# Weight sums of a block-matrix scheme: made on VectorE in SBUF, or by adding transfers in DRAM

## The chip, the cores and the metric

The kernel runs on one core of one Trainium2 chip. Five engines run side by side, each through its own list of instructions in order: TensorE (PE: matmul; PEld: its weight loads), VectorE (DVE), ScalarE (ACT), GpSimd (POOL) and SyncE (SP), which here issues transfers only. Transfers (DMA) are carried out by 16 DMA engines, which all issuing engines share. The metric is the device time of one execution in microseconds (us), lower is better.

## The reference

One layer of an encoder over 2048 tokens of width 1024, all float32: chunked softmax attention with 16 heads of 64, then a SwiGLU feed-forward of width 2816, each between two RMS norms.

```python
def reference(x, g_pre_mix, g_post_mix, w_qkv, w_o, rel_bias, g_pre_ffn, g_post_ffn, w_gate, w_up, w_down):
    for i in range(DEPTH):                      # DEPTH = 1
        h = rms_norm(x, g_pre_mix[i])
        m = chunk_relpos_attention(h, w_qkv[i], w_o[i], rel_bias[i // N_MIXERS])
        x = x + rms_norm(m, g_post_mix[i])
        h = rms_norm(x, g_pre_ffn[i])
        x = x + rms_norm(swiglu(h, w_gate[i], w_up[i], w_down[i]), g_post_ffn[i])
    return x

def swiglu(h, w_gate, w_up, w_down):
    return (jax.nn.silu(h @ w_gate) * (h @ w_up)) @ w_down
```

In the attention, a chunk of 64 tokens reads its own and the eight chunks before it, with a learned bias by head and clipped distance added to the scores.

## The kernel before

Tokens are worked in two groups of 1024 (`g`), each of two halves of 512 (`s`). Every dense product is made of three matmuls (`products`, L188 to L190): each operand is split into a rounded part `hi` and a remainder `lo`, and hi·hi + hi·lo + lo·hi are added up in PSUM.

The feed-forward multiplies by a seven-product scheme for 2×2 block matrices: seven block products in place of eight. It needs four sums of the weights' blocks A11, A21, A22, A12, called S1 to S4, once per unit of weights. There are 17 units: eleven of the gate and up matrices, six of the down matrix, one of these of half width. Activations get sums of the same kind (T1 to T4), and the products are put together by further adds (`gate_up`, `down`).

The weight sums don't depend on the tokens, so they are made early, while the attention runs (first 1100 us), and are stored in DRAM (`sum_gu`, `sum_d`), from which the feed-forward loads them (L862, L880). One unit before the change: SyncE loads the four blocks into SBUF (`ws_A...`, L817), VectorE makes four sums in place (L820), SyncE stores the four results (L829).

What sets the order: TensorE's list is written out by hand. For each pair of heads `p` and each half `s` there is an `Attend` job of four slots (128 queries each). In a slot TensorE makes the scores of both heads into one PSUM bank `st` (L521, L522), VectorE adds the bias and finds the extreme (L530, out of the bank, which is then free for the next slot), ScalarE takes the exponential (L534), VectorE the reciprocal (L537), GpSimd normalises (L538), and TensorE transposes the result a slot later (L554, L565). Between these pieces dense matmuls (the q, k, v and output projections) are put in by a planner (`fill`). The other engines' lists are set by the framework's scheduler, from the order in which the program is written and its own estimate of when each instruction is ready.

The bias of a head is a tile of 128×640 that SyncE loads (L420) and in which GpSimd overwrites two corners (L421, L422). There are three such buffers and a pair of heads needs two, so the second tile of each pair can be loaded only when the pair before has made its last scores. Attention outputs are copied to one of three `io` tiles and stored by SyncE (L590).

The dense weights of the attention come in slabs: `fetch` (L119 on) loads slab `n` in two halves (`raw`, L139, one buffer) and splits it on ScalarE and VectorE. `take` hands out a slab and fetches the next. Behind the loads of certain slabs (`UNIT_AT`: 3 to 11 and 22 to 31) one unit of weight sums is written into the program.

Of the kernel before, what the change touches and what calls it, by code (L numbers as in the profile page):

```python
# [47 lines left out]
def trunk(  # L48
# [71 lines left out]
    def fetch():  # L120
        n = len(ready)
        if n == len(plan):
            return
        tiles = [w_tile(f"{n}_{c}") for c in range(2)]
        raw = None
        if n in roomy:

            raw = phase["ap"].tile([P, 4 * HALF], F32, tag="q", name=f"raw_{n}", bufs=2)
            sp.dma_start(raw, plan[n])
        for c in range(2):  # L130
            here = slice(c * 1024, c * 1024 + 1024)
            if n in roomy:
                part, ins = raw[:, here], None
            else:
                if "fp" in phase:
                    part = phase["fp"].tile([P, 1024], F32, tag="w4", name=f"raw_{n}_{c}", bufs=4)
                else:
                    part = wp.tile([P, 1024], F32, tag="raw", name=f"raw_{n}_{c}", bufs=1)
                ins = sp.dma_start(part, plan[n][:, here])  # L139
# [348 lines left out]
    class Attend:  # L488
# [14 lines left out]
        def scores(self, ib):  # L503
# [19 lines left out]
            for h in range(2):  # L523
# [14 lines left out]
                pool.tensor_scalar(  # L538
# [146 lines left out]
    class Blocks:  # L685
# [45 lines left out]
        def first(self, w):  # L731
# [28 lines left out]
        def all(self, w):  # L760
# [13 lines left out]
            def two(k):  # L774
                b11, b12, b22, b21 = c[k]
                t3 = narrow("t3")
                dve.tensor_tensor(t3, b22, b12, op=ALU.subtract)
                dve.tensor_tensor(b12, b12, b11, op=ALU.subtract)
# [3 lines left out]
            def three(k):  # L782
                b11, b12, b22, b21 = c.pop(k)
                dve.tensor_tensor(b22, b22, b12, op=ALU.subtract)
# [26 lines left out]
    def weight_sums(src, dst):  # L811

        t = {}

        def load(n):
            t[n] = phase["ap"].tile(list(src[n].shape), F32, tag="ws", name=f"ws_{n}", bufs=4)
            sp.dma_start(t[n], src[n])  # L817

        def add(out_, a, b, op):
            dve.tensor_tensor(t[out_], t[a], t[b], op=op)  # L820
# [5 lines left out]
        steps = [(0.5, lambda n=n: load(n)) for n in ("A11", "A21", "A22", "A12")]  # L826
        steps += [(2.0, lambda a=a: add(*a)) for a in sums]
        for n, at in (("S1", "A22"), ("S3", "A21"), ("S2", "A11"), ("S4", "A12")):
            steps.append((0.5, lambda n=n, at=at: sp.dma_start(dst[n], t[at])))  # L829
        return steps  # L830

    def gate_up_sums(c):
        return weight_sums({n: w_gu[c, BLOCK_AT[n]] for n in BLOCK_AT}, {n: sum_gu[n][:, c, :] for n in sum_gu})

    def down_sums(c):
        def at(t):
            return t[:, c, :] if c == 0 else t[:, c : c + 2, :].rearrange("p a b -> p (a b)")

        return weight_sums({n: at(w_d[BLOCK_AT[n]]) for n in BLOCK_AT}, {n: at(sum_d[n]) for n in sum_d})
# [57 lines left out]
    def gate_up(g, b):  # L897
# [20 lines left out]
        for c in range(NC):  # L918
# [21 lines left out]
            def closing(pts, terms, then):  # L940
                def go(i):
                    dve.tensor_tensor(terms[i], pts[i], terms[i], op=ALU.add)  # L942
# [8 lines left out]
            def sub(n, a, b_, to=None):  # L951
                t[n] = narrow(n) if to is None else to
                dve.tensor_tensor(t[n], a, b_, op=ALU.subtract)

            def c12(x_):
                t["B12"] = x_
                sub("T1", x_, t["B11"])
                put("T1")

            def c22(x_):  # L960
                t["B22"] = x_
                put("B22")
                sub("T3", x_, t["B12"], t["B12"])
                put("T3")
                sub("T2", x_, t["T1"])
                put("T2")

            def c21(x_):
                t["B21"] = x_
                put("B21")  # L970
                sub("T4", x_, t["T2"])
# [9 lines left out]
            yield from product(pc, "B22", False, closing(pc, u2, c12))  # L981
# [8 lines left out]
    def down(g, store, between=lambda n: None):  # L990
# [45 lines left out]
        def add(a, b_):  # L1036
            return lambda dst: dve.tensor_tensor(dst, a, b_, op=ALU.add)
# [17 lines left out]
        def u(d, _):  # L1055
            if not end:
                u2[d] = narrow("u2")
            dve.tensor_tensor(u2[d], pc[d], p1[d], op=ALU.add)
# [10 lines left out]
        def c22(d, _):  # L1069
            dve.tensor_tensor(u3[d], pc[d], p1[d], op=ALU.add)  # L1070
            store(1, 4 + d, whole, add(u3[d], p5[d]))
# [261 lines left out]
    units.extend(gate_up_sums(c) for c in range(NC))  # L1333
    units.extend(down_sums(c) for c in [0] + list(range(1, NC, 2)))
# [125 lines left out]
```

## Time and profile before

| what | value |
|---|---|
| time, median of 3 runs | 2495.56 us (2490.86 to 2497.91) |
| profiled execution: its time / its span | 2493.5 us / 2491.6 us |
| granted TensorE clock, mean | 0.990 |
| TensorE busy | 2418.1 us (97%) |
| VectorE busy | 1595.5 us (64%) |
| GpSimd busy | 328.7 us (13%) |
| weight sums on VectorE (L820) | 68 instructions, 85.5 us, from 90.4 to 927.4 us |
| their transfers (L817, L829) | 68 loads, 68 stores, all but 8 of 512 KB |
| DMA engines | 52.9% busy, 441.21 MB moved |

The profile is one execution, recorded by the hardware's profiler. Busy time of TensorE is partly modelled (matmuls are pipelined), so what counts is where it is idle and what it waited for. A row of a stretch gives for each engine the busy microseconds and the number of instructions, then the granted clock, the busy share of the DMA engines and GB/s. A row in order of time gives start, duration, engine, line, operation, out<-in, and in brackets the idle time just before it and who ended it.

### The profile page before, as it was taken

How to read it: one execution, taken by the hardware profiler on the slowest of the kernel's cores; microseconds unless marked ns; L12 is line 12 of the kernel's file. 1: busy time of each engine (PE TensorE's matmuls, PEld its weight loads, DVE VectorE, ACT ScalarE, POOL GpSimd, SP SyncE). 2: the span in 40 equal slices, each digit the busy share in tenths (PEclk: the TensorE clock that was granted, in tenths of full speed). 3: DMA queues.
4: the chain of work that ended last, by engine and by line, in shares of the span. 5: the costliest groups of instructions: out<-in, count | busy, mean ns of one | idle time of the engine just before them, and what ended most of it. 6: DMA issues, size and time to landing. Idle time of an engine off the chain costs nothing.

```text
span 2491.6 us, 34707 instructions
## 1 busy us (share of the span) xinstructions
PE 2418.1 (97%) x12536; PEld 1998.1 (80%) x12536; DVE 1595.5 (64%) x2698; ACT 1145.0 (46%) x1979; POOL 328.7 (13%) x428
## 2 busy tenths in 40 slices
PE   7999999999999999999999999999999999999997
PEld 5787877778878787877888788888888888888886
DVE  6766675658676755577666656577656655555576
ACT  5555554654565535464533243356443333334443
POOL 3232232211322222220000000000000000000002
PEclk9999999999999999999999999999999999999998
DMA  4545353445545441137666755377667664457653
GB/s 143 206 151 207 119 201 130 142 157 187 201 149 182 162 158 47 60 116 236 199 196 227 245 182 181 102 241 247 209 219 260 198 204 154 135 169 244 193 191 134
DMA packets 184316, 441.21 MB, mean 177 GB/s; under 512 B 20272, under 2 KB 22336, under 8 KB 182864
## 3 DMA queue, kind: packets, MB, share of 16 engines
q1 hardware_dynamic: 184144, 438.99, 52.9%
q8 instruction: 99, 1.62, 0.3%
q14 instruction: 73, 0.60, 0.1%
HBM read 325.09 MB, written 113.82 MB: 176 GB/s over the span
## 4 chain that ended last, share of the span: by engine, by line
PE 52%; DMA 1%; DVE 1%; issue 0%; ACT 0%; POOL 0%; SPq 0%; POOLq 0%; DVEq 0%; ACTq 0%
PE pd L189 5%; PE pd L188 5%; PE pd L190 5%; PE pb L188 5%; PE pb L189 5%; PE pb L190 5%; PE pa L188 3%; PE pa L189 3%; PE pa L190 3%; PE pc L188 3%; PE pc L189 3%; PE pc L190 3%; PE mm L188 1%; PE mm L190 1%; PE mm L189 1%; DMA res<-in_x 1%
## 5 line engine op out<-in xcount | busy, mean ns | idle before, releaser
L188 PE MATMUL mm<-hb,whi 128*128 128x512 f32 x720 | 299.2, 415 | 2.9 <-ACT hb L340 2.4
L534 ACT ACTIVATE sc<-sc,nmax 128x640 f32<-128x640 f32 (+4 forms) x256 | 193.5, 757 | 211.1 <-DVE nmax L530 208.8
L189 PE MATMUL mm<-hb,whi 128*128 128x512 f32 x720 | 284.5, 395 | 1.5 <-DVE hb L341 0.9
L190 PE MATMUL mm<-hb,wlo 128*128 128x512 f32 x720 | 284.8, 396 | 0.0
L538 POOL TENSOR_SCALAR sc<-sc,rows 128x640 f32<-128x640 f32 (+4 forms) x256 | 204.3, 802 | 595.5 <-DVE rows L537 545.8
L530 DVE CUSTOM_DVE_ANT_0 sc<-st,bias 128x640 f32<-128x640 f32 (+4 forms) x256 | 181.1, 736 | 79.6 <-PE st L522 73.0
L188 PE MATMUL pb<-hb,whi_gu_T 128*128 128x512 f32 x528 | 206.7, 391 | 2.1 <-DVE terms L942 2.1
L189 PE MATMUL pb<-hb,whi_gu_T 128*128 128x512 f32 x528 | 206.2, 390 | 0.0
L190 PE MATMUL pb<-hb,wlo_gu_T 128*128 128x512 f32 x528 | 206.0, 390 | 0.0
L258 POOL TENSOR_TENSOR rs<-ms,neg_half 128x4 f32<-128x4 f32 (+1 forms) x12 | 19.5, 1622 | 1222.8 <-DVE ms L256 1222.7
L188 PEld LDWEIGHTS mm<-hb,whi 128*128 128x128 f32 x720 | 136.8, 190 | 38.1 <-issue 14.7
L190 PEld LDWEIGHTS mm<-hb,wlo 128*128 128x128 f32 x720 | 136.3, 189 | 30.0
L189 PEld LDWEIGHTS mm<-hb,whi 128*128 128x128 f32 x720 | 137.0, 190 | 24.3 <-DVE hb L341 2.5
L521 PE MATMUL st<-k,q 128*128 128x384 f32 (+1 forms) x448 | 132.5, 316 | 17.3 <-DVE nmax L530 14.5
L188 PE MATMUL mm<-whi,hb 128*128 128x256 f32 x480 | 143.4, 299 | 0.0
L189 PE MATMUL pd<-a,whi_d_T 128*128 128x512 f32 (+1 forms) x368 | 140.0, 380 | 0.7 <-DVE a L341 0.7
L188 PE MATMUL pd<-a,whi_d_T 128*128 128x512 f32 (+1 forms) x368 | 140.1, 381 | 0.1
L190 PE MATMUL pd<-a,wlo_d_T 128*128 128x512 f32 (+1 forms) x368 | 139.8, 380 | 0.0
L188 PE MATMUL pa<-hb,whi_gu_B 128*128 128x512 f32 x352 | 137.5, 391 | 1.1 <-ACT terms L923 1.1
L190 PE MATMUL pa<-hb,wlo_gu_B 128*128 128x512 f32 x352 | 137.0, 389 | 0.0
L189 PE MATMUL pa<-hb,whi_gu_B 128*128 128x512 f32 x352 | 137.0, 389 | 0.0
L190 PE MATMUL mm<-whi,hb 128*128 128x256 f32 x480 | 136.7, 285 | 0.0
(219 smaller groups left out, 5842.7 us busy)
## 6 DMA issues: line engine op xcount, KB each, us to landing
raw<-gu_S SPq DMA_DIRECT2D x88, 512.0 KB, 3.8
raw<-in_w_gu SPq DMA_DIRECT2D x66, 512.0 KB, 4.1
y<-y SPq DMA_DIRECT2D x96, 256.0 KB, 3.7
ws_A<-in_w_gu SPq DMA_DIRECT2D x44, 512.0 KB, 6.8
gu_S<-ws_A SPq DMA_DIRECT2D x44, 512.0 KB, 3.0
raw_a<-aT SPq DMA_DIRECT2D x88, 256.0 KB, 3.6
raw_d<-d_S SPq DMA_DIRECT2D x88, 256.0 KB, 3.5
raw<-in_w_a SPq DMA_DIRECT2D x40, 512.0 KB, 4.3
```

Of the source, the lines that this page charges most:

```text
L188: pe.matmul(pt, a_hi, b_hi, start=first, stop=False, skip_group_check=go_on)
L189: pe.matmul(pt, a_hi, b_lo, start=False, stop=False, skip_group_check=go_on)
L190: pe.matmul(pt, a_lo, b_hi, start=False, stop=last, skip_group_check=go_on)
L258: pool.tensor_tensor(r[0][:, :nb], m[:, :nb], neg_half.to_broadcast([P, nb]), op=ALU.pow)
L521: pe.matmul(st[:, a:b], q[:, h, cols], kk[:, h, key], start=True, stop=False)
L530: dve.tensor_tensor_reduce(out=sc[:, :n], in0=st[:, c0 : c0 + n], in1=rev, scale=-1.0, scalar=3.0e38, op0=ALU.add, op1=ALU.min, accum_out= ...
L534: act.activation(sc[:, :n], sc[:, :n], AF.Exp, bias=nmax, scale=-1.0, accum_out=rows[:, 0:1])
L538: pool.tensor_scalar(sc[:, :n], sc[:, :n], rows[:, 1:2], 1.0, op0=ALU.mult, op1=ALU.mult)
```

## The change

The sums are no longer made on VectorE. Per unit SyncE copies four blocks from DRAM to DRAM straight into the places of the sums (S1 ← A21, S2 ← A11, S3 ← A11, S4 ← A12), and GpSimd issues four transfers that add a block to what lies there (S1 += A22, S3 += A21, then S2 += S1, then S4 += S2). An adding transfer can only add, so the scheme's signs are turned: S3 was A11 − A21 and is A11 + A21, S2 was S1 − A11 and is S1 + A11, S4 was A12 − S2 and is A12 + S2; the activations' sums T1, T2 and T3 and several of the closing adds take the other sign. The blocks of the weights in DRAM are the same, and so are the number and the operands of VectorE's adds and subtracts of the activations.

The adds of unit `n − 1` (S1, S3), `n − 2` (S2) and `n − 3` (S4) are issued with the copies of unit `n`, so each comes at least one fetch after what it reads. `tc.issue_after(last_pool[0].ins)` places them behind the last normalisation written so far on GpSimd. The copies have no such tie. The slabs after which a unit is written are now 3 to 12 and 20 to 29. The scratch space for GpSimd's transfers grows from 256 to 1024 bytes per partition.

```diff
         ready.append(tiles)
-        if units and n in UNIT_AT:
-            with tc.issue_after(ins.ins):
-                for _, step in units.popleft():
-                    step()
-    UNIT_AT = set(range(3, 12)) | set(range(22, 32))
-    units = deque()
+        if n in SUMS_AT:
+            weight_sums(SUMS_AT.index(n))
+    SUMS_AT = list(range(3, 13)) + list(range(20, 30))
+    last_pool = [None]
...
-                pool.tensor_scalar(
+                last_pool[0] = pool.tensor_scalar(
...
-                dve.tensor_tensor(t3, b22, b12, op=ALU.subtract)
-                dve.tensor_tensor(b12, b12, b11, op=ALU.subtract)
-                dve.tensor_tensor(b22, b22, b12, op=ALU.subtract)
+                dve.tensor_tensor(t3, b12, b22, op=ALU.subtract)
+                dve.tensor_tensor(b12, b11, b12, op=ALU.subtract)
+                dve.tensor_tensor(b22, b22, b12, op=ALU.add)
                 dve.tensor_tensor(t4, t4, b22, op=ALU.subtract)
...
-    def weight_sums(src, dst):
-        t = {}
-        def load(n):
-            t[n] = phase["ap"].tile(list(src[n].shape), F32, tag="ws", name=f"ws_{n}", bufs=4)
-            sp.dma_start(t[n], src[n])
-        def add(out_, a, b, op):
-            dve.tensor_tensor(t[out_], t[a], t[b], op=op)
-        sums = (
-            ("A22", "A21", "A22", ALU.add), ("A21", "A11", "A21", ALU.subtract),
-            ("A11", "A22", "A11", ALU.subtract), ("A12", "A12", "A11", ALU.subtract),
-        )
...
+    units = [gate_up_at(c) for c in range(NC)] + [down_at(c) for c in range(0, NC, 2)]
+    def weight_sums(n):
+        def add(u, *pairs):
+            if 0 <= u < len(units):
+                src, dst = units[u]
+                for to, a in pairs:
+                    with tc.issue_after(last_pool[0].ins):
+                        pool.dma_start(dst[to], dst[a] if a in dst else src[a], accum_op=ALU.add)
+        add(n - 1, ("S1", "A22"), ("S3", "A21"))
+        add(n - 2, ("S2", "S1"))
+        add(n - 3, ("S4", "S2"))
+        if n < len(units):
+            src, dst = units[n]
+            for to, a in (("S1", "A21"), ("S2", "A11"), ("S3", "A11"), ("S4", "A12")):
+                sp.dma_start(dst[to], src[a])
...
             def u(i):
-                dve.tensor_tensor(u2[i], pb[i], p1[i], op=ALU.add)
+                dve.tensor_tensor(u2[i], p1[i], pb[i], op=ALU.subtract)
...
-    nc = bacc.Bacc("TRN2", target_bir_lowering=False, num_devices=1, dynamic_dma_scratch_size=256)
+    nc = bacc.Bacc("TRN2", target_bir_lowering=False, num_devices=1, dynamic_dma_scratch_size=1024)
```

How this moves instructions is seen in the engines' lists. On SyncE, before the change, the end of the third unit, up to two bias loads, of the second tile of the third pair and the first of the fourth (`raw`: weight slab, `gu_S`: place of a finished sum, `ws_A`: block in SBUF, `kh`: keys kept for the next group, `attn`: attention output):

```order
L486 DMA kh_0_121<-k_2_1302 256x1x512
L829 DMA gu_S_147<-ws_A_1493 128x1024
L829 DMA gu_S_149<-ws_A_1491 128x1024
L829 DMA gu_S_148<-ws_A_1489 128x1024
L139 DMA raw_0_1966<-in_w_a 128x1024
L829 DMA gu_S_150<-ws_A_1495 128x1024
L590 DMA attn_0_88<-ot 128x512
L420 DMA bias_1819<-ext_d 128x640
L420 DMA bias_2385<-ext_d 128x640
```

And now, up to the first of the same two bias loads (`d_S`: place of a sum of the down matrix):

```order
L139 DMA raw_0_1935<-in_w_a 128x1024
L835 DMA d_S_152<-in_w_d 128x1024
L835 DMA d_S_153<-in_w_d 128x1024
L588 DMA attn_0_88<-ot 128x512
L835 DMA d_S_154<-in_w_d 128x1024
L835 DMA d_S_151<-in_w_d 128x1024
L835 DMA d_S_152<-in_w_d 128x1024
L835 DMA d_S_153<-in_w_d 128x1024
L835 DMA d_S_154<-in_w_d 128x1024
L835 DMA d_S_151<-in_w_d 128x1024
L835 DMA d_S_152<-in_w_d 128x1024
L418 DMA bias_1788<-ext_d 128x640
```

At a place where three units had been begun before, the copies of the last units (`d_S`) are being issued: nine between the slab's half and the bias load, where one store stood. Counted over the list, 11 copies stand before the second half of slab 2, 51 from there to this bias load, and 6 behind it.

On GpSimd, the same time, normalisations (`sc`) and the corners of a bias tile, before:

```order
L538 TENSOR_SCALAR sc<-sc,rows 128x640
L421 MEMSET bias_1819 64x64
L422 MEMSET bias_1819 64x64
L538 TENSOR_SCALAR sc<-sc,rows 128x640
L421 MEMSET bias_2385 64x64
L422 MEMSET bias_2385 64x64
L538 TENSOR_SCALAR sc<-sc,rows 128x128 x2
L538 TENSOR_SCALAR sc<-sc,rows 128x256 x2
L538 TENSOR_SCALAR sc<-sc,rows 128x384 x2
```

And now, a little further on in the same list:

```order
L419 MEMSET bias_2338 64x64
L420 MEMSET bias_2338 64x64
L536 TENSOR_SCALAR sc<-sc,rows 128x128 x2
L536 TENSOR_SCALAR sc<-sc,rows 128x256 x2
L827 DMA gu_S_147<-in_w_gu 128x1024
L827 DMA gu_S_149<-in_w_gu 128x1024
L827 DMA gu_S_148<-gu_S_147 128x1024
L827 DMA gu_S_150<-gu_S_148 128x1024
L536 TENSOR_SCALAR sc<-sc,rows 128x384 x2
```

A batch of four adds, of the third, second and first units, stands between the normalisations of two slots. TensorE's list is the same as before, instruction by instruction.

More of the change, by code (lines that the diff above doesn't have):

```diff
@@ L132, in fetch @@
             if n in roomy:
-                part, ins = raw[:, here], None
+                part = raw[:, here]
             else:
@@ L1057, in u @@
                 u2[d] = narrow("u2")
-            dve.tensor_tensor(u2[d], pc[d], p1[d], op=ALU.add)
+            dve.tensor_tensor(u2[d], p1[d], pc[d], op=ALU.subtract)
         yield from product(pc, True, u)
@@ L1069, in c22 @@
         def c22(d, _):
-            dve.tensor_tensor(u3[d], pc[d], p1[d], op=ALU.add)
-            store(1, 4 + d, whole, add(u3[d], p5[d]))
+            dve.tensor_tensor(u3[d], pc[d], p1[d], op=ALU.subtract)
+            store(1, 4 + d, whole, add(u3[d], p5[d], ALU.subtract))
         yield from product(pc, False, c22)
```

48 lines of the change are left out of this document (20 added, 28 removed).

## The prediction

> **What bounds the kernel now.** I read the page first: engines, then the chain that ended last.
>
> ```profile
> span 2491.6 us, 34707 instructions
> PE 2418.1 (97%) x12536; PEld 1998.1 (80%) x12536; DVE 1595.5 (64%) x2698; ACT 1145.0 (46%) x1979; POOL 328.7 (13%) x428
> PE 52%; DMA 1%; DVE 1%; issue 0%; ACT 0%; POOL 0%; SPq 0%; POOLq 0%; DVEq 0%; ACTq 0%
> ```
>
> TensorE is busy for 2418.1 of 2491.6 us, and no change here touches a matmul. So whatever VectorE loses is worth only what it takes out of TensorE's 73.5 us of idle time, and the question is where that idle time lies. The busy time by stretch answers: sums are made from about 76 to 500 us and from 617 to 932 us; from 932 to 1100 us the same attention runs without them.
>
> ```profile
> core 0: us, PE busy (x) PEld busy (x) DVE busy (x) ACT busy (x) POOL busy (x), PEclk, DMA share, GB/s
> 76.00:200.00 124.00, 117.57 (x735) 97.61 (x735) 77.71 (x181) 64.47 (x139) 38.37 (x54) 1.00 0.49 174
> 200.00:500.00 300.00, 287.14 (x1753) 235.40 (x1752) 194.43 (x432) 163.79 (x340) 81.49 (x126) 0.98 0.45 161
> 617.00:932.00 315.00, 300.38 (x1924) 251.39 (x1922) 211.30 (x421) 165.72 (x312) 89.18 (x115) 0.98 0.47 170
> 932.00:1100.00 168.00, 166.86 (x1055) 137.66 (x1057) 103.74 (x228) 94.90 (x182) 48.36 (x66) 1.00 0.22 72
> ```
>
> TensorE's idle time is 6.4, 12.9 and 14.6 us in the three stretches with sums (length less PE busy), and 1.1 us of 168 (0.7%) in the one without. What it waited for there, from the list of waits, and one such wait in the order of time:
>
> ```profile
> PE st L521 <- DVE nmax L530: 14.5, 10, 2.7
> PE pssq L254 <- DVE total L240: 8.1, 3, 5.9
> PE tt L565 <- DVE pT L557: 4.0, 6, 2.1
> ...
> 236.41 1.23 DVE L820 TENSOR_TENSOR ws_A<-ws_A,ws_A 128x1024 f32<-128x1024 f32 x1
> 237.55 0.16 DVE L537 RECIPROCAL rows<-rows 128x1 f32<-128x1 f32 x1
> 237.62 0.67 DVE L557 COPY pT<-tt 128x512 f32<-128x512 f32 x1
> 238.21 1.22 DVE L820 TENSOR_TENSOR ws_A<-ws_A,ws_A 128x1024 f32<-128x1024 f32 x1
> 239.34 0.28 DVE L530 CUSTOM_DVE_ANT_0 sc<-st,bias 128x128 f32<-128x128 f32 x1
> ...
> 239.69 0.39 PE L521 MATMUL st<-k,q 128*128 128x256 f32 x1 [2.08 <-DVE nmax L530]
> ```
>
> Two sums of 1.2 us each sit on VectorE ahead of the score's reduction (L530), and TensorE's next score matmul waits 2.08 us for the bank. Such a wait costs again in the granted clock:
>
> ```profile
> 238.00:242.00 4.00, 2.31 (x11) 1.31 (x13) 4.00 (x8) 0.49 (x2) 1.42 (x4) 0.90 1.00 395
> 242.00:246.00 4.00, 4.00 (x24) 1.97 (x22) 1.31 (x7) 1.09 (x4) 1.41 (x3) 0.67 0.95 350
> 872.00:876.00 4.00, 0.71 (x4) 0.72 (x4) 4.00 (x6) 1.55 (x3) 0.29 (x2) 0.59 0.78 320
> 876.00:880.00 4.00, 4.00 (x20) 4.00 (x20) 1.79 (x6) 0.92 (x2) 1.82 (x2) 0.50 0.88 273
> 880.00:884.00 4.00, 4.00 (x24) 4.00 (x23) 0.71 (x3) 1.19 (x2) 0.80 (x1) 0.63 0.76 281
> ```
>
> After 2.08 us of idling the clock (third column from the right) is 0.90 and 0.67 for 4 us each, 0.4 + 1.3 = 1.7 us lost; after the 5.9 us wait of the list, 0.50 and 0.63 while TensorE is full, 2.0 + 1.5 = 3.5 us.
>
> **What goes away.** 68 sums on VectorE (L820, 85.5 us by its row below) and what they delay. Beyond 200 us that is at most 12.9 + 14.6 us less 0.7% of 615 us (4.2), 23 us, and the clock's 0.02 of 615 us, 12 us: 35 us. The lower end is 15, since some of this idling has other owners. I take 29. The 5.6 us before 200 us are counted apart, for a reason that comes next. The reversed signs put an add for a subtract on the same operands, with no instruction more: nothing. After 1100 us nothing moves: the loads of finished sums stay.
>
> **What is added: SyncE's copies.** The order shows what the diff doesn't: the copies from DRAM to DRAM wait for no engine's work, so they are not spread over the time of the units; all 68 stand in SyncE's queue ahead of the store of the fourth attention output. Eleven come early, before the weight load at 67.22 us, and have landed by then; 51 stand between the weight load at 67.22 us and the bias load that SyncE issues at 176.18 us; the last six (four of half size) come just behind that.
>
> ```profile
> 67.22 0.33 SPq L139 DMA_DIRECT2D raw<-in_w_a  x1
> 176.18 2.98 SPq L420 DMA_DIRECT2D bias<-ext_d  x2
> 178.26 0.80 POOL L538 TENSOR_SCALAR sc<-sc,rows 128x640 f32<-128x640 f32 x1 [1.62 <-DVE rows L537]
> 179.61 0.14 POOL L421 MEMSET bias<- 64x64 f32 x1 [0.55 <-DMA bias<-ext_d]
> ...
> 180.43 0.80 POOL L538 TENSOR_SCALAR sc<-sc,rows 128x640 f32<-128x640 f32 x1 [0.48 <-DVE rows L537]
> ...
> DMA to landing us min/median/max: 3.2/4.5/9.0
> ```
>
> That bias load has no room: GpSimd stands waiting for it at 179.61 us with the second head's normalisation (180.43 us) queued behind, for which TensorE's transposes wait. The last row (of the bias tile's view) has 9.0 us as the worst landing so far: behind four loads of sums. What a copy costs the 16 queues isn't in this trace. What loads give at best is:
>
> ```profile
> 124.00:126.00 2.00, 1.59 (x8) 0.97 (x7) 1.97 (x4) 1.89 (x4) 0.00 (x0) 1.00 1.02 417
> 154.00:156.00 2.00, 2.00 (x20) 2.00 (x19) 1.97 (x5) 1.95 (x4) 0.39 (x1) 1.00 1.04 424
> ws_A<-in_w_gu SPq DMA_DIRECT2D x44, 512.0 KB, 6.8
> gu_S<-ws_A SPq DMA_DIRECT2D x44, 512.0 KB, 3.0
> L820 DVE TENSOR_TENSOR ws_A<-ws_A,ws_A 128x1024 f32<-128x1024 f32 (+1 forms) x68 | 85.5, 1257 | 7.0 <-DMA ws_A<-in_w_gu 5.8 <-DMA ws_A<-in_w_d 0.8
> ```
>
> 424 GB/s with the queues full (share 1.04) makes 1.25 us for a transfer of 512 KB that crosses the DRAM's side once. A copy crosses it twice. Lower end 1.25 us, if reading and writing overlap fully; upper end 3.0 us, the whole landing of a lone store. I take two crossings, 2.5 us, and for an add (reads two blocks, writes one) three, 3.75 us: every row shows this total, reads and writes together, topping out near 420. The Trainium skill, page "DMA: Bandwidth & Descriptors", section "Latency and other measured facts", gives 207 to 214 GB/s per direction for copies between DRAM tensors, an estimate of 2.5 us a block from that page, with which the sum would be the same; no run here shows it yet.
>
> The sum for 67 to 176 us: 51 copies, 127.5 us; 17 other transfers that stand there anyway (12 of 512 KB, 3 of 256, 2 of 320, so 14.75 blocks), 18.4 us; the 5 adds due by then, 18.8 us. That is 165 us of transfers in a queue that must be through by about 181 us, 114 us later. So 51 us are missing, and TensorE stands still for about 50, parted over two or three places: the second bias tile of each new pair of heads, and an attention output's store whose buffer is needed again. The idling before 200 us is swallowed by this. With 1.25 us (adds too) the need is 88 us and nothing stalls; with 3.0 us (adds 4.5) it is 194, and 80 us stall. Weight loads are late too, but a slab is fetched while the one before it is multiplied, some 42 us (ten slabs in the 424 us from 76 to 500), which is more than the ten or so by which a burst delays one. The clock after three long stalls, at 1.7 to 3.5 us each: 7.5.
>
> **What is added: GpSimd's issues.** Batches of four adds stand behind a pair of normalisations. One issue costs between 0.33 us (SyncE's, quoted above) and 1.6 us (GpSimd's dearest small instruction), so a batch takes 1.3 to 6.5 us.
>
> ```profile
> L538 POOL TENSOR_SCALAR sc<-sc,rows 128x640 f32<-128x640 f32 (+4 forms) x256 | 204.3, 802 | 595.5 <-DVE rows L537 545.8 <-PE tt L554 26.6 <-PE po L583 9.4
> L258 POOL TENSOR_TENSOR rs<-ms,neg_half 128x4 f32<-128x4 f32 (+1 forms) x12 | 19.5, 1622 | 1222.8 <-DVE ms L256 1222.7
> ...
> 311.08 1.42 POOL L538 TENSOR_SCALAR sc<-sc,rows 128x512 f32<-128x512 f32 x2 [4.46 <-PE tt L554]
> ...
> 316.44 1.04 PE L554 MATMUL tt<-ident,sc 128*128 128x128 f32 x8
> ```
>
> The cover is GpSimd's idling before a pair (595.5 / 128 = 4.7 us) and the 3.9 us from the pair's end at 312.50 to its transposes at 316.44. 8.6 us hide 6.5; I take 2 us in all for tight pairs. Without this cover each microsecond over would cost 17, one per batch. Queued behind an add are the normalisations and bias memsets; an add's own wait is for transfers issued a fetch before.
>
> **The sum.** 2493.5 (the profiled execution) − 29 + 50 + 7.5 + 2 = 2524. The three runs have their median 2 us higher, so I say 2525.
>
> **Rivals.** (a) A copy costs what a load costs, 1.25 us. For it: loads read DRAM and write SBUF at once at 424, so an engine does overlap. Against it: no row shows more than that across the DRAM's side. Then no stall, and the early 5.6 us are won as well: 2493.5 − 29 − 5.6 + 2 + 2 = 2463; with only half of the idling gone, 2480. It decides below 1.63 us a copy, where 58.5 copies' worth (51 and five adds at one and a half) fit into 114 − 18.4 = 95.6 us. (b) Between: at 1.9 us a copy 16 us stall, with two clock dips 5: 2493.5 − 29 + 16 + 5 + 2 + 2 = 2490, no change. (c) With copies cheap as in (a), GpSimd is held by each issue beyond any row, at 3 us: a batch takes 12, 3.4 over the cover, 17 times 58 us: 2463 + 58 = 2521. For it: no add was ever issued here. Against it: GpSimd waits for VectorE in nearly every idle row, so it is early. The Trainium skill, page "SBUF — State Buffer", section "Who interferes with whom", has GpSimd's descriptor writing blocked while VectorE holds the shared port in a two-port mode, which would lengthen these issues; no run here shows it yet.
>
> **How the numbers follow.** Forecast 0.55, (a) 0.26, (b) 0.11, (c) 0.08. The forecast's own range, for 2.2 to 2.8 us a copy (33 to 68 us stalled), is 2506 to 2545. For 8 in 10 it must reach into (a) and allow for still slower adds: 2465 to 2552. About 0.3%, 7.5 us, is what can be told from no change. Faster: most of (a) and a little of (b), 0.27; the same: most of (b) and some of (a), 0.10; slower: the forecast and (c), 0.63.
>
> **What would show it.** Right: TensorE idle for 10 us or more at a time between 110 and 190 us, released by the reduction L528 (now) or GpSimd behind a bias load that took 10 to 20 us to land; DMA share near 1 there; after 200 us less idling than now, clock 1.00. A burst of copies landing every 2.5 us confirms the price, every 1.3 us refutes it, and with it the forecast. Transposes waiting for GpSimd right behind adds, all through to 930 us, would be (c). Gaps unchanged after 200 us would say that the sums were not what TensorE waited for.

## The result, and the profile after

| | median | range | ratio to before, 95% interval |
|---|---|---|---|
| before, same chip | 2493.73 us | 2483.9 to 2497.91, 6 runs | |
| the change | 2506.53 us | 2505.49 to 2513.25, 6 runs | 1.0067 [1.0052, 1.0082] |

The change makes the kernel slower, by 13 to 17 us (medians; ratio times 2493.7). The forecast was 2525 us, slower, with a range of 2465 to 2552. The sign was right, but the loss arose elsewhere than forecast: the stretch from 500 to 617 us, of which the prediction did not speak, has cost about as much as the whole net loss.

The page of the profiled execution, its engines and its fullest DMA queues:

```profile
span 2503.7 us, 34587 instructions
...
PE 2417.1 (97%) x12536; PEld 1998.1 (80%) x12536; DVE 1523.9 (61%) x2630; ACT 1142.8 (46%) x1979; POOL 368.7 (15%) x496
...
q1 hardware_dynamic: 174352, 404.38, 49.5%
q0 software_dynamic: 9792, 34.61, 7.6%
```

VectorE is 72 us less busy, GpSimd 40 us more, and a queue of GpSimd's own (q0) has appeared. The busy time by stretch, with the columns of the prediction's table (the granted clock third from the right):

```profile
76.00:200.00 124.00, 111.77 (x688) 93.34 (x688) 60.10 (x160) 59.71 (x130) 38.49 (x60) 0.94 0.93 298
200.00:500.00 300.00, 286.02 (x1755) 235.53 (x1754) 165.76 (x406) 160.84 (x337) 98.79 (x151) 0.98 0.50 128
500.00:617.00 117.00, 102.62 (x471) 83.19 (x472) 69.63 (x110) 56.27 (x96) 16.37 (x21) 0.91 0.65 192
617.00:932.00 315.00, 309.81 (x2033) 261.20 (x2031) 193.50 (x407) 167.34 (x316) 106.85 (x141) 1.00 0.47 119
```

TensorE's idle time from 76 to 200 us has gone from 6.4 to 12.2, from 200 to 500 us from 12.9 to 14.0, and from 617 to 932 us from 14.6 to 5.2. Only this last stretch has kept its gain. The stretch from 500 to 617 us idles 14.4 us at a clock of 0.91, where it idled 1.2 us before:

```profile
500.00:617.00 117.00, 115.78 (x608) 97.24 (x606) 83.38 (x130) 59.10 (x100) 15.31 (x14) 1.00 0.53 176
```

Three waits tell most of it. TensorE's list of waits:

```profile
PE mm L186 <- ACT y L237: 11.7, 1, 11.7
PE tt L563 <- DVE pT L555: 10.7, 9, 6.8
PE tt L552 <- POOL sc L536: 9.6, 4, 6.9
```

And the same places in order of time, with SyncE's issues:

```profile
185.41 0.14 POOL L419 MEMSET bias<- 64x64 f32 x1 [9.43 <-DMA bias<-ext_d]
185.59 0.29 DVE L528 CUSTOM_DVE_ANT_0 sc<-st,bias 128x128 f32<-128x128 f32 x1 [7.64 <-POOL bias L419]
...
186.72 1.11 PE L552 MATMUL tt<-ident,sc 128*128 128x128 f32 x4 [6.91 <-POOL sc L536]
...
411.82 0.14 POOL L419 MEMSET bias<- 64x64 f32 x1 [7.75 <-DMA bias<-ext_d]
...
413.67 0.69 PE L563 MATMUL tt<-ident,sc 128*128 128x128 f32 x2 [6.82 <-DVE pT L555]
...
517.81 1.70 POOL L827 DMA_DIRECT2D gu_S<-in_w_gu  x2
518.90 1.45 POOL L827 DMA_DIRECT2D gu_S<-gu_S  x1
...
525.14 0.81 POOL L827 DMA_DIRECT2D gu_S<-gu_S  x1 [4.79 <-issue]
526.40 5.69 SPq L288 DMA_DIRECT2D prep<-in_x  x8
528.87 0.84 POOL L827 DMA_DIRECT2D gu_S<-in_w_gu  x1 [2.92 <-issue]
532.93 0.82 POOL L827 DMA_DIRECT2D gu_S<-in_w_gu  x1 [3.22 <-issue]
...
535.01 0.63 ACT L233 ACTIVATE prep<-prep 128x512 f32<-128x512 f32 x1 [8.06 <-DMA prep<-in_x]
...
547.96 0.63 ACT L237 ACTIVATE sq<-prep 128x512 f32<-128x512 f32 x1 [2.09 <-DMA prep<-in_x]
548.49 0.58 ACT L237 ACTIVATE y<-mm 128x512 f32<-128x512 f32 x1
...
549.12 0.79 PE L186 MATMUL mm<-hb,whi 128*128 128x512 f32 x1 [11.70 <-ACT y L237]
```

At 180 and at 407 us GpSimd waits for a bias tile that landed 11 us after its issue, the first behind copies and adds, the second behind adds. At 537 us two batches of adds (eight, back to back) meet the eight loads of the second group's tokens (`prep`, 256 KB each). The last row of the tile's view, for the change and then for the kernel before:

```profile
DMA to landing us min/median/max: 8.5/17.7/20.5
```

```profile
DMA to landing us min/median/max: 3.2/5.9/7.7
```

ScalarE works on these tokens one load after another, and an instruction that empties a result bank (`y<-mm`, 548.49 us) stands behind them in its list. TensorE waits 11.7 us for it, and the clock is 0.50 to 0.54 for 18 us from 544 us on.

### The profile page after: what moved, and what is told of

It is laid out like the page before. It is cut to its first block, busy times and chain, and to the rows that moved or that the text cites. A ratio compares the mean times of both kernels' runs of the same rounds, so it can differ in the third digit from the quotient of the medians.

```text
span 2503.7 us, 34587 instructions
## 1 busy us (share of the span) xinstructions
PE 2417.1 (97%) x12536; PEld 1998.1 (80%) x12536; DVE 1523.9 (61%) x2630; ACT 1142.8 (46%) x1979; POOL 368.7 (15%) x496
## 3 DMA queue, kind: packets, MB, share of 16 engines
q0 software_dynamic: 9792, 34.61, 7.6%
HBM read 359.69 MB, written 148.42 MB: 203 GB/s over the span
## 4 chain that ended last, share of the span: by engine, by line
PE 51%; DMA 2%; DVE 1%; issue 0%; ACT 0%; POOL 0%; SPq 0%; POOLq 0%; DVEq 0%; ACTq 0%
PE pd L187 5%; PE pd L186 5%; PE pd L188 5%; PE pb L186 4%; PE pb L187 4%; PE pb L188 4%; PE pa L186 3%; PE pa L187 3%; PE pa L188 3%; PE pc L186 3%; PE pc L188 3%; PE pc L187 3%; PE mm L186 1%; PE mm L188 1%; PE mm L187 1%; DMA y<-y 0%
## 5 line engine op out<-in xcount | busy, mean ns | idle before, releaser
L186 PE MATMUL mm<-hb,whi 128*128 128x512 f32 x720 | 300.2, 417 | 14.6 <-ACT y L237 11.7
L536 POOL TENSOR_SCALAR sc<-sc,rows 128x640 f32<-128x640 f32 (+4 forms) x256 | 200.3, 797 | 519.4 <-DVE rows L535 478.0
L186 PEld LDWEIGHTS mm<-hb,whi 128*128 128x128 f32 x720 | 137.3, 191 | 50.2 <-issue 14.6
```

The costliest lines, as they stand in the source:

```text
L186: pe.matmul(pt, a_hi, b_hi, start=first, stop=False, skip_group_check=go_on)
L536: last_pool[0] = pool.tensor_scalar(sc[:, :n], sc[:, :n], rows[:, 1:2], 1.0, op0=ALU.mult, op1=ALU.mult)
```

## The experiments

Every ratio stands against runs of the kernel before on the same chip, whose medians there lie between 2490.41 and 2492.98 us.

| kernel | median, us | ratio to before, 95% interval |
|---|---|---|
| batches later (`late`) | 2492.39 | 0.9999 [0.9988, 1.0010] |
| copies tied (`tied`) | 2526.87 | 1.0133 [1.0112, 1.0154] |
| both (`tied_late`) | 2521.16 | 1.0108 [1.0090, 1.0127] |
| before without VectorE's sums (`no_vector_sums`) | 2498.08 | 1.0029 [1.0016, 1.0041] |
| four bias buffers (`bias4`) | 2492.95 | 1.0003 [0.9993, 1.0013] |
| batches later, four bias buffers (`late_bias4`) | 2477.85 | 0.9935 [0.9913, 0.9957] |
| the same with twice the scratch (`late_bias4_ring`) | 2471.61 | 0.9932 [0.9918, 0.9945] |
| before without any sums (`no_sums`) | 2454.01 | 0.9849 [0.9830, 0.9869] |
| GpSimd's transfers as plain copies (`plain_pool`) | 2478.98 | 0.9955 [0.9940, 0.9970] |
| before, additions kept, their transfers cut (`thin`) | 2489.41 | 0.9994 [0.9985, 1.0004] |
| one at a time, four bias buffers (`slots_bias4`) | 2466.53 | 0.9905 [0.9892, 0.9919] |
| the change without adds (`copies_only`) | 2461.43 | 0.9876 [0.9857, 0.9895] |

**Is the wait at 537 us the batches' doing?**

```diff
-    SUMS_AT = list(range(3, 13)) + list(range(20, 30))
+    SUMS_AT = list(range(3, 12)) + list(range(22, 33))
```

> The change with its units written behind slabs 3 to 11 and 22 to 32 instead of 3 to 12 and 20 to 29: no batch of adds is issued while the kernel passes from the first group of tokens to the second (500 to 617 us), and the copies stay where they are. Theory (the 17 us lost at 510 to 565 us come from two batches of adds that meet the loads of the second group's tokens): the gap of 11.7 us in front of the second group's first matmuls falls below 2 us, the clock there stays at 1.00, and the kernel is about 16 us faster than the change, near 2490, no change against before. Rival (that gap has another owner, such as the norm at the group's start being placed later): the gap stays at 10 us or more and the time at 2505. Second rival (the batches moved to the end find the same trouble later): the gap goes and another of its size appears between 930 and 1000 us.

Measured: 0.9999 against the change's 1.0067, 17 us less. The stretch of the passage between the groups, in this kernel:

```profile
500.00:617.00 117.00, 114.88 (x593) 95.53 (x592) 85.79 (x136) 63.68 (x108) 13.97 (x16) 1.00 0.50 168
```

The idling is 2.1 us instead of 14.4, the clock 1.00, and `prep` lands in 5.5 us. No new gap of that size stands further on. The theory holds, in place and size (17 us against 16).

**Is the copies' burst the loss up to 240 us?** Here the four copies of a unit are placed behind the slab's load.

```diff
-            for to, a in (("S1", "A21"), ("S2", "A11"), ("S3", "A11"), ("S4", "A12")):
-                sp.dma_start(dst[to], src[a])
+            with tc.issue_after(ins.ins):
+                for to, a in (("S1", "A21"), ("S2", "A11"), ("S3", "A11"), ("S4", "A12")):
+                    sp.dma_start(dst[to], src[a])
```

> The change with each unit's four copies placed behind the load of the weight slab with which they are written, so that they are no longer run ahead of in SyncE's queue. Theory (the copies' burst makes the bias loads late, 10 to 15 us with the clock dips behind it): TensorE's gap of 6.9 us near 180 us and the short ones at 112 and 128 us go, the DMA engines' share between 110 and 190 us falls from 1.0 to 0.7 or less, and the time falls by 10 to 15 us, to about 2493. Rival (the adds alone delay the loads): the gap near 180 us stays at 5 us or more and the time within 3 us of the change's.

> Both edits: copies behind their slab's load, and no batch between 500 and 617 us. Theory (two separate losses of about 15 us each, and a gain of 15 us that the change does bring from 617 us on): the two add up, about 30 us below the change, near 2476, which is 0.7% faster than before. Rival (the two are one queue's trouble, and the copies moved back come to collide with the adds further on): less than 15 us below the change, 2491 or more, with new gaps behind batches of adds between 200 and 500 us.

Measured: 1.0133 and 1.0108, both slower than the change (16 and 10 us). The theory fell. Each unit's copies are now in the queues at about the time of a batch of adds, time after time through the attention. One of the waits of `tied`:

```profile
776.00 1.68 POOL L827 DMA_DIRECT2D d_S<-in_w_d  x2
777.08 1.43 POOL L827 DMA_DIRECT2D d_S<-d_S  x1
787.91 0.83 POOL L827 DMA_DIRECT2D d_S<-d_S  x1 [9.40 <-issue]
788.45 0.45 POOL L419 MEMSET bias<- 64x64 f32 x1
...
790.02 0.69 PE L519 MATMUL st<-k,q 128*128 128x384 f32 x1 [8.32 <-DVE nmax L528]
```

The bias tile lands at 784.2 us, 11.8 us after its issue. Its corners are written only at 788.45, since the fourth add stands in front of them on GpSimd and is issued only when the first add has landed, at 787.6. TensorE waits 8.32 us. Having the copies out of the way early, which the hoisting does, was an advantage of 16 us.

**What can taking the sums from VectorE bring?** Three kernels made from the one before. The first leaves out VectorE's additions only, the second everything that makes sums, the third the transfers (to 16 columns of 1024) but not the additions.

```diff
-        steps += [(2.0, lambda a=a: add(*a)) for a in sums]
```

> The kernel before without its 68 sums on VectorE: the blocks are loaded and stored unsummed with the same transfers, so that the feed-forward is computed from unsummed blocks. It bounds what taking the sums from VectorE can bring. Theory (my step one: the sums and the clock dips behind them are what TensorE waits for): 29 us below before, up to 35, and TensorE's idle time from 617 to 932 us falls from 14.6 to 4 us or less. Rival (half of that idling has other owners, as the 15 us gained by the change from 617 us on suggest): 15 to 20 us below before. Second rival (the transfers, not the sums, are what delays): within 8 us of before.

```diff
-        if units and n in UNIT_AT:
+        if False:
```

> The kernel before with no weight sums at all: neither their loads and stores nor VectorE's additions, and the feed-forward loads a block of the weights where it loaded a sum, with transfers of the same size and number. So the sums of the reference's scheme are left out, and the time is the floor for any way of making them. Theory (loads and stores of the sums in SyncE's queue, rather than VectorE's additions, are what makes TensorE wait in the kernel before, because a bias load stands behind four of them): 20 to 30 us below before, near 2468, with TensorE's idle time from 617 to 932 us below 4 us. Rival (neither sums nor their transfers own that idling): within 8 us of before. My prediction's step one, that VectorE's additions own it, would give the same fall here, but has failed in the kernel that left out the additions alone.

```diff
-            sp.dma_start(t[n], src[n])
+            sp.dma_start(t[n][:, :16], src[n][:, :16])
...
-            steps.append((0.5, lambda n=n, at=at: sp.dma_start(dst[n], t[at])))
+            steps.append((0.5, lambda n=n, at=at: sp.dma_start(dst[n][:, :16], t[at][:, :16])))
```

> The kernel before with all 68 sums still made on VectorE (same size, on four tiles kept in SBUF), but with their loads and stores cut from 1024 columns to 16, and the feed-forward loading blocks where it loaded sums. So the sums made aren't those of the reference. Together with the kernel that left out the additions alone and the one that left out both, it tells what VectorE's part is. Theory (the transfers, through late bias loads, own TensorE's idling; VectorE's additions hardly any): within 10 us of the kernel without any sums, 2454 to 2464, and idle time from 617 to 932 us of 5 us or less. Rival (my prediction's step one, VectorE's additions own it): 2480 or more, with gaps released by the score's reduction behind sums.

Measured: without the additions 1.0029, without either 0.9849 (38 us below before), with the additions alone 0.9994. Two stretches of the kernel without either, and then the same two of the kernel with additions and hardly any transfers:

```profile
200.00:500.00 300.00, 296.95 (x1841) 244.31 (x1840) 171.17 (x416) 167.82 (x349) 78.22 (x130) 1.00 0.28 94
...
617.00:932.00 315.00, 312.63 (x2001) 260.25 (x2000) 185.13 (x408) 173.22 (x329) 89.58 (x124) 0.99 0.22 71
```

```profile
200.00:500.00 300.00, 289.37 (x1761) 237.35 (x1759) 193.91 (x434) 164.22 (x342) 87.09 (x126) 0.98 0.26 80
...
617.00:932.00 315.00, 304.01 (x1959) 255.60 (x1960) 213.89 (x427) 168.85 (x320) 90.71 (x118) 0.99 0.25 74
```

After the first kernel the theory was that the transfers own the idling, not VectorE; it fell with the third. The additions alone, at half the DMA share, cost 0.9994 less 0.9849, 1.45% or 36 us; the kernel before loses 38 us against the same floor. So the sums on VectorE are enough to explain the idling of before. The two prices do not add up, though: the transfers alone cost 1.0029 less 0.9849, 45 us. The place that the prediction quoted at 239 us looks as follows with hardly any transfers (L825 is the sum there):

```profile
239.86 1.22 DVE L825 TENSOR_TENSOR ws_A<-ws_A,ws_A 128x1024 f32<-128x1024 f32 x1
241.00 0.28 DVE L530 CUSTOM_DVE_ANT_0 sc<-st,bias 128x128 f32<-128x128 f32 x1
...
241.21 1.22 DVE L825 TENSOR_TENSOR ws_A<-ws_A,ws_A 128x1024 f32<-128x1024 f32 x1
...
242.75 0.39 PE L521 MATMUL st<-k,q 128*128 128x256 f32 x1 [3.47 <-DVE nmax L530]
```

And without the additions, at the same matmul:

```profile
229.88 2.68 SPq L828 DMA_DIRECT2D gu_S<-ws_A  x3
232.62 1.20 SPq L420 DMA_DIRECT2D bias<-ext_d  x1
...
238.88 0.14 POOL L421 MEMSET bias<- 64x64 f32 x1 [8.99 <-DMA bias<-ext_d]
...
239.41 0.58 PE L521 MATMUL st<-k,q 128*128 128x256 f32 x1 [8.20 <-DVE nmax L530]
```

Nothing holds the stores back any more, so they stand in front of the bias load, which before was issued ahead of them (229.14 us, landing at 238.14). The same order stands at 732 us, in front of a wait of 7.0 us at 740. The kernel meant to remove one cause has set free another of the same size. It does not bound the gain; `no_sums` does.

**Which transfers cost what?** The change without adds, and the change with GpSimd's transfers as plain copies:

```diff
-        add(n - 1, ("S1", "A22"), ("S3", "A21"))
-        add(n - 2, ("S2", "S1"))
-        add(n - 3, ("S4", "S2"))
```

> The change without its 68 adds: the copies run as they do there, hoisted to the front of SyncE's queue, and what lies in the sums' places is one block of each sum. It prices the burst of copies alone, against the kernel without any sums (2454). My prediction's term (a copy occupies the DMA engines for 2.5 us, 51 us are missing before the bias load near 176 us): with the adds' 18.8 us taken off its sum, 32 us of stall and 2484 or more. Theory now (copies land every 1.5 us, and the burst delays a bias load and short transfers by 11 us): gaps of 2 to 3 us near 112 us and 5 to 7 us near 180 us stay, those at 212, 407 and 537 us go, 10 to 15 us above the floor, 2464 to 2469. Rival (the copies alone always land in time, and the gaps up to 200 us are the first adds' doing as well): within 5 us of the floor, under 2459.

```diff
-                        pool.dma_start(dst[to], dst[a] if a in dst else src[a], accum_op=ALU.add)
+                        pool.dma_start(dst[to], dst[a] if a in dst else src[a])
```

> The change with GpSimd's 68 transfers as plain copies of the same blocks from the same places, without adding (the sums are then single blocks): it prices the adding by itself. Theory (an add reads two blocks and writes one, so it occupies the DMA engines for about twice a copy): the batch in front of the second group's first matmuls lands a transfer every 1.5 us instead of every 3.2 to 3.7, that gap falls from 11.7 to 5 us or less, and the time is 12 to 20 us below the change's, near 2490. Rival (what is slow is GpSimd's queue, with descriptors written one transfer at a time, whatever they do): landings stay 3 us apart and the time within 4 us of the change's.

Measured: 0.9876 and 0.9955. The copies alone are 0.27% (7 us) above the floor, less than the theory's 10 to 15: no wait is left at 180 us, where the two bias tiles land in 5.4 and 5.8 us. So the change's wait there needs the adds as well. With plain copies on GpSimd's queue the time is 28 us below the change, more than the theory's 12 to 20; that it is the queue, whatever the transfers do, is refuted. A stretch of this burst, and then GpSimd's queue in the kernel with plain copies:

```profile
92.00:98.00 6.00, 6.00 (x35) 5.25 (x34) 4.78 (x12) 4.72 (x12) 2.12 (x3) 1.00 0.99 369
```

```profile
q0 software_dynamic: 9536, 34.61, 4.1%
```

With the queues full of copies, 369 GB/s make 1.42 us for 512 KB. The landings bear out that a copied byte counts once: three copies land at 76.84, 78.08 and 79.32 us, and from 93.81 to 99.72 us one lands every 1.35 to 1.6 us. GpSimd's queue moves 34.61 MB, 66 transfers of that size: 4.1% of 2474.7 us is 1.54 us each as copies, and 7.6% of 2503.7 us (the change) is 2.88 us each as adds. That is 1.87 times as much time of packets for the same bytes. The plain copies also take GpSimd less time to issue (0.52 against 0.88 us in the median), and none of them is held as the adds are (see the larger ring below). The Trainium skill, page "Collectives: The Full Stack", section "The bandwidth ceiling: the fold count and why AG ≠ RS ≠ AR", says of the adding transfers of a reduce-scatter that they read two sources through the same ring and so run at half of a copy's rate, 1.93 as measured there. This trace agrees in the time. The second read itself does not show: the profile's page counts 359.69 MB read from DRAM with adds and with plain copies alike.

The distance of the n-th matmul's start from the same matmul's in the kernel without sums, in us, worked out from the traces (up to there TensorE's order is the same in all; the start is that in the kernel without sums):

```
matmul  its start  before  thin  copies_only  plain_pool  change  late_bias4  slots_bias4
   900      170.1     8.6   9.2          5.6         6.1     5.5         8.6          1.6
  1650      286.0    13.0  16.0          6.1        13.0    22.4        19.7          5.2
  2700      456.2    21.2  21.2          6.4        18.1    31.9        19.5          5.3
  3300      576.9    25.5  24.8          9.5        25.6    50.9        20.4          6.7
  5100      857.6    40.9  34.8          9.6        24.9    51.9        21.8         12.5
```

Before loses a little everywhere; the change loses 51 us by 577 us and then about 1 us. The copies' own part is 9.6 us here, 6.6 at the last matmul, and 7 by the ratios.

**What is late in the bursts?** A fourth buffer lets both bias tiles of a pair be loaded a pair ahead.

```diff
-        t = phase["ap"].tile([P, 640], F32, tag="bias", name=f"bias{h}", bufs=3)
+        t = phase["ap"].tile([P, 640], F32, tag="bias", name=f"bias{h}", bufs=4)
```

> The change with four bias buffers in place of three, in room that VectorE's sums have left, so that both tiles of a pair of heads can be loaded a whole pair ahead. Theory (TensorE's gaps of 6.9 us at 180 and 6.8 us at 407 us are a bias load that sits behind a burst of copies or adds and lands 11 us after its issue): both gaps fall below 2 us, the clock dips behind them go, the gap of 11.7 us at 537 us stays, and the kernel is 14 to 18 us faster than the change, near 2490. Rival (something else is as late in the same bursts: a weight slab, or a normalisation behind GpSimd's fourth add): other gaps of 4 us or more stand at the same places, and the time falls by less than 8 us.

> The change with four bias buffers and with no batch of adds between 500 and 617 us. Theory (two separate losses, of which the second was measured at 14 us): they add up, 28 to 32 us below the change, near 2476, which is 0.6 to 0.8% faster than before. Rival (bursts only move their damage to whatever is late next): 2485 or more.

Measured: 1.0003, 16 us below the change, and 0.9935 with the later batches, 33 us below it: the two losses add up (17 + 16). The waits at 180 and 407 us are gone. But up to 500 us not all is well, as two stretches of `late_bias4` show:

```profile
76.00:200.00 124.00, 116.14 (x723) 96.78 (x722) 63.33 (x167) 62.60 (x137) 40.98 (x63) 0.99 0.98 306
200.00:500.00 300.00, 288.42 (x1777) 237.86 (x1776) 168.51 (x413) 165.71 (x345) 97.24 (x148) 0.99 0.46 122
```

19.4 us idle against 3.6 without sums. Two waits have grown: 4.7 us at 124 us, where GpSimd writes the corners of a tile that is needed only later, waits for its load, and has normalisations queued behind, and 6.95 us at 205 us, where a weight slab lands 14.0 us after its issue, behind adds.

**One at a time, and a larger ring.** In `slots_bias4`, in six of eight slots of the attention, one copy is issued behind SyncE's latest transfer and one add behind the latest normalisation. It has the fourth bias buffer too, and no add is issued between 423 and 601 us:

```diff
-        if n in SUMS_AT:
-            weight_sums(SUMS_AT.index(n))
...
+        if slot % 8 > 5 or slot // 8 > 6:
+            return
+        if copies:
+            u, to, a = copies.popleft()
+            with tc.issue_after(last_sp[0].ins):
+                nc.sync.dma_start(units[u][1][to], units[u][0][a])
+        if n_sums[0] >= 8 and adds:
+            u, to, a = adds.popleft()
+            src, dst = units[u]
+            with tc.issue_after(last_pool[0].ins):
+                pool.dma_start(dst[to], dst[a] if a in dst else src[a], accum_op=ALU.add)
+        n_sums[0] += 1
...
+                weight_sums(t + 1)
```

> The change with four bias buffers, and with copies and adds given out one at a time: in six of each eight slots of the attention one copy is issued behind SyncE's latest transfer and one add behind GpSimd's latest normalisation, so that there are no bursts and none between 500 and 617 us. Theory (what is left in the kernel with late batches and four bias buffers, 19 us idle from 76 to 500 us against 4 us without sums, comes from bursts, of copies up to 200 us and of adds): 8 to 14 us below that kernel, 2464 to 2470, about 1% faster than before. Rival (one add at a time still makes every transfer behind it late by 3 us and the fixed total of transfers sets the loss): within 4 us of it, 2474 to 2482, with many gaps of 1 to 2 us in place of a few long ones.

```diff
-    nc = bacc.Bacc("TRN2", target_bir_lowering=False, num_devices=1, dynamic_dma_scratch_size=1024)
+    nc = bacc.Bacc("TRN2", target_bir_lowering=False, num_devices=1, dynamic_dma_scratch_size=2048)
```

> The change with late batches and four bias buffers, and with 2048 instead of 1024 bytes of scratch for GpSimd's transfers. In the change the fourth add of a batch is issued only when the first has landed. Theory (the scratch holds three transfers, and the fourth one's wait keeps normalisations and bias corners behind it): all four adds of a batch are issued within 6 us of each other, GpSimd's idle time in front of its adds that nothing but the issue explains falls from 59 to under 10 us, and the time falls by 2 to 5 us from 2478. Rival (GpSimd is early enough, and the fourth add issued sooner takes more of the DMA engines at once from the loads): no change or up to 5 us slower.

Measured: 0.9905 [0.9892, 0.9919], 24 us faster than before and the fastest of all that make every sum. Against `late_bias4`, which differs in how the transfers are given out, that is 7 us, just under the theory's 8 to 14 and clear of noise by little. Its first stretches:

```profile
76.00:200.00 124.00, 122.27 (x765) 102.66 (x764) 68.13 (x178) 69.56 (x149) 41.91 (x66) 1.00 0.54 147
200.00:500.00 300.00, 294.52 (x1822) 241.93 (x1822) 170.47 (x417) 166.63 (x346) 97.54 (x156) 0.99 0.70 184
```

7.2 us idle, and the transfers are parted between the two stretches: DMA shares of 0.54 and 0.70, where `late_bias4` has 0.98 and 0.46. The longest wait there is 1.9 us. Of the gaps of 1 to 2 us that the rival expected in great number there are six from 200 to 932 us; three of them (at 264, 677 and 805 us) have no counterpart of 1 us or more in `no_sums` and `copies_only`.

The larger ring does what the theory said to GpSimd and nothing measurable to the time (0.9932 against 0.9935); the 2 to 5 us that the theory forecast are less than these runs can tell. The add's line in the change has this row, which has no counterpart with 2048 bytes:

```profile
  issue: 58.9, 17
```

## Why the prediction was right on the sign and wrong in its parts

Each term of the sum, against the ratios above times 2493.7 us. The intervals are some 0.1 to 0.2% each, so a difference of two is good to 3 to 6 us.

| term | forecast | measured |
|---|---|---|
| gain from VectorE's sums | −29 | −38 with their loads and stores (floor 0.9849); −36 by the additions alone |
| copies | 32 of the 51 us missing, with clock dips behind | +7 |
| adds, as transfers on GpSimd's queue | 19 of the 51, and 2 for issues | +20 |
| adds, because they add | (in the same 19) | +28 |
| sum | +31 | +17 |

**The gain** was found by the right reading: the sums stand in front of the score's reduction, and the clock pays again. It was taken too small on two counts. By the starts of its matmuls, the kernel before loses 33 us to the floor between 200 and 1100 us, where the forecast had 35 in view and put 6 down to other owners. And it loses 8.6 us up to 200 us, which the forecast counted as swallowed by a stall that did not come.

**The price of a copy** is the step that failed. "Two crossings, 2.5 us", on the ground that every row's total tops out near 420 GB/s: that total counts a byte copied once, as the 369 GB/s of the copies show, and 1.42 us is near the lower end of 1.25 that was kept for rival (a). With the measured prices the prediction's own need from 67 to 181 us is 72 us of copies, 18 of other transfers and 14 of adds: 105 of the 114 us there, and no stall of 50 us. The hoisting into SyncE's queue, which the order showed, is real and costs 7 us by itself. By its own test (landings every 2.5 us confirm, every 1.3 refute) the forecast's first pillar is refuted. Of its other signs, the bias load that takes 10 to 20 us to land came (11.2 us), but no idle time of 10 us or more between 110 and 190 us did (the longest is 6.9), and after 200 us only the stretch from 617 us on idles less than before. The 207 to 214 GB/s for copies between DRAM tensors that the prediction cited from the Trainium skill (page "DMA: Bandwidth & Descriptors", section "Latency and other measured facts") lie far below the 369 GB/s that the copies of this case reach; the page measured them on tensors with 512 KiB or a padded 4 MiB from row to row, another layout than that of the gate and up blocks here (4 KB in the weights, 44 KB in the sums).

**The adds** were priced in the right region (3.75 us forecast; 2.88 us of all 16 engines, 3.1 to 4.1 us from one landing to the next in the batches at 525 us), but only the five that fall before 181 us were put into a sum. The others were called free once GpSimd's issue was covered. What the prediction asked of them was whether GpSimd is late; what decides is what their transfers make late: bias tiles, slabs, and above all the tokens of the second group, 17 us of the loss by `late` alone. These sit on SyncE's queue, in another place of the program than the adds' issues. Of the 52 us that the change loses to the kernel without sums, 36 arise between 200 and 617 us (15.3 at 200, 50.9 at 617), where the forecast had only GpSimd's issues, 2 us.

**Rival (a)** had the copies nearly right and the adds wrong: its 2463 is nearly the time without adds (2461), in part by luck, since it has 3 us less gain, no price for the copies and 4 us for adds, which that kernel leaves out. **Rival (c)** named something that exists: in front of 17 adds GpSimd is held 58.9 us in all, 3.5 us each, since the scratch holds three adds. But its price of 58 us is not there: with the hold gone the time moves by less than the 6 us that can be told. **The signs** were costed at nothing; no kernel tried them alone, and the stretch from 1100 us on, where the turned signs are used, moves the change by 0.4 us in the end and some 2 us on the way against the kernel without sums (51.9 us at matmul 5100, 52.3 at the last).

So two errors of 25 us or more had opposite signs, and the time came out within the range partly by luck. The sign did too: with the copies at their measured 7 us, the forecast's other terms (−29, and 21 for the adds) add up to no change. It is the adds, priced at less than half of what they cost, that make the kernel slower.

## What to carry to other kernels

Work that is moved from an engine into transfers is not priced when its issue is hidden: ask for every load that shares the DMA engines how much later it lands, and where its reader has slack, above all where the program passes from one phase to the next. Keep such transfers away from those loads, and give them out one at a time: the same 136 transfers cost 54 us in bursts (1.0067 less 0.9849) and 14 us spread (0.9905 less 0.9849). Of these 40 us, 33 were won by one more buffer for the load that had no slack and by keeping the adds out of the passage between the groups, the other 7 by spreading the rest. And when a suspected cause is taken out, look whether the order behind it has changed: the floor came from removing both causes, not one.

## What the runs showed of the hardware that was not expected

- A transfer from DRAM to DRAM of 512 KB costs 1.42 us with the queues full (369 GB/s; 1.46 and 1.55 us in two later stretches of the burst, at 359 and 339 GB/s), not twice a load's 1.25 us.
- The packets of an adding transfer take 1.87 times as long as those of a copy of the same block (2.88 against 1.54 us of all 16 engines), and its issue on GpSimd takes 0.81 to 1.46 us against a median of 0.52.
- While adds run, loads of another queue come in step with them. From 532 to 545 us in the change adds land at 532.6, 535.9, 539.0, 542.3 and 545.4 us, and the token loads of 256 KB at 534.9, 538.2, 541.4 and 544.7. The Trainium skill, page "DMA: Bandwidth & Descriptors", section "Queues, rings and completion order", has each DMA engine take turns between the queues, a packet at a time; that would give such a step, and no run here tests it apart. With plain copies in place of the adds the step is there too, at the copies' pace: copies land at 517.8, 519.7, 521.6 and 523.5 us, token loads at 519.4, 521.2 and 523.2.
- With 1024 bytes of scratch per partition three adds are in flight, and the fourth is issued when the first has landed (525.14 us against 524.83). With 2048 bytes no such hold is left.
- With a stand of 11.7 us goes a clock of 0.50 to 0.54 for 18 us (544 to 562 us), 12 of them after TensorE has started again; the prediction had counted 8 us of dips behind a wait of 5.9 us.
